# The convolution branch's output projection as four Strassen pairs instead of sixteen plain products

## The chip, the cores and the metric

One Trainium2 chip; the kernel runs on one of its cores. The metric is the device time of one execution in microseconds (us); the time given for a kernel is the median of its runs. One further execution is recorded by the hardware profiler, which logs the instructions of each engine and the transfers. Engines: PE (TensorE, matrix products), PEld (its weight loads), DVE (VectorE), ACT (ScalarE), POOL (GpSimd), SP (SyncE, which issues nearly all transfers here).

## The reference, cut to what matters

One encoder block on 1024 tokens with 1024 channels in fp32: two branches, each gated and projected, then merged.

```python
h = rmsnorm(x, norm_w) * (1 + scale) + shift          # [1024 tokens, 1024]
proj = h @ w_in                                       # all branches at once
ya = a_cg * dwconv_centred(a_bg * a_x, conv_a_w)      # convolution branch, width 3
ya = ya * silu(a_z)
ya = ya @ w_pa                                        # the first output projection, "pa"
...                                                   # yb: gated DeltaNet over q, k, v with z
yb = yb @ w_pb                                        # the second, "pb"
merged = sigmoid(gate_a_raw) * ya + sigmoid(gate_b_raw) * yb
x = x + gate * (merged @ w_o)                         # gate: from c @ w_ada, "output gate"
out = rmsnorm(x, final_norm_w)
```

## The kernel before, in words

Everything is kept transposed: a channel block of 128 channels lies on the 128 partitions, the 1024 tokens along the free axis. A matrix product in fp32 is made of three passes in the format fp32r: each operand t is split into hi = round(t) (a copy on ACT) and lo = t - hi (a subtraction on DVE or POOL), and PE adds whi*rhi + whi*rlo + wlo*rhi in PSUM. One such pass for 128 output channels, 128 contraction channels and 512 tokens is one instruction, "a matmul" below.

**Stages.** Up to about 757 us a planner (`sched.run`) orders the gated DeltaNet heads with the projections that feed them. After that the text below is program order on each engine, for ACT, DVE, POOL and SP, until the context `sctx` closes; PE runs its products in the order written too. In turn come the convolution branch in sixteen pairs, the rest of the gate of the second branch (`gb`: two pairs, then `gate_block` 6 and 7 as plain products), pa as plain products, pb as plain products, and the final projection with `w_o`.

**A plain product** (`product`) is 8 contraction blocks by 3 passes = 24 matmuls for one output block and 512 tokens.

**A pair** (class `Pair`) computes two output blocks j0 and j0+1 for both token halves with seven products in place of eight, by Strassen's scheme in Winograd's form. Its weight operands are four quarters `A11, A12, A21, A22` (output block by half of the contraction; the halves are the even and the odd channel blocks, `KORDER`) and their sums `S1` to `S4` (`ADDS`); its right-hand operands are `B11, B21, B22` of h and the sums `T1` to `T4` of h (`RHS`), which stand ready in `hop`. A product is 4 blocks by 3 passes = 12 matmuls, so a pair is 84 instead of 96. `load` fetches the four raw quarters (names `wr_...`), `operand` forms the sums on DVE, `prep` makes hi on ACT, `rest` makes lo on DVE, `product` issues the matmuls, and `after` issues what follows a product: `u2`, `u3`, `e1` are copies or sums of PSUM banks in SBUF, and `consume` takes a finished quarter of the result. S2, S3 and A22 add up in one PSUM bank (pool `pg`), S1 and S4 in one of `pc`, A11 and A12 each have one of `pp`. S3 may add to the bank only after u2 has been read from it, A22 only after u3 has.

**The order of pairs.** `steps` lists pairs bg, ax, cg, az for j0 = 0, 2, 4, 6 and then gb2, gb4, seven products each. In the ordinary order (S2, A11, S1, S3, A12, A22, S4) a pair begins with S2; the first pair has the order A11, A12, S4, S2, S1, S3, A22, the last one S2, S3, S1, A22, A11, A12, S4. In step i the loop issues the loads of the pair of step i+10, `prep` for step i+5, `rest` for step i+4, then the product of step i, then one operation from the list `late`: the three taps of the width-3 convolution per channel block. The early operands and the first two products of bg0 stand in the planner's part (`ps_first_A11`, `ps_first_A12`).

**The channel blocks of ya.** After az, `a` holds a finished block of the branch (`conv * silu(a_z) * a_cg`); it is stored to `y_d` in DRAM. At four steps before the end of the list all eight blocks are fetched into `ylo` and split into `yhi`, `ylo` around gate blocks 6 and 7.

**pa** runs over j = 0..7: weights by `wtile` (hi on ACT, lo on POOL), two products, a multiplication with the stored gate `sga` on DVE, and a store to `m_d`. The same loop fetches the second branch's `yb_d` into `blo`, splits it into `bhi`, `blo`, and forms the output gate: a `tensor_tensor_reduce` on DVE per j, with a fetch of 512 KB of `wadag`.

**pb** runs over j = 0..7: two products, the gate `sgb`, the addition of `m_d`, the split of the result.

Of the kernel before, what the change touches and what calls it, by code (L numbers as in the profile page):

```python
# [8 lines left out]
F32 = mybir.dt.float32  # L9
# [6 lines left out]
P = 128  # L16
# [311 lines left out]
def block(ctx: ExitStack, tc: tile.TileContext, x, c, wada, wadag, badaT, nwT, win, wab, cva, cvq,  # L328
# [860 lines left out]
    def fill():  # L1189
# [100 lines left out]
    class Pair:  # L1290
# [36 lines left out]
        def rest(self, n):  # L1327
            if len(self.ops[n]) < 3:
                return
            hi, lo, t = self.ops[n]  # L1330
            V.tensor_tensor(lo, t, hi.bitcast(F32), ALU.subtract)

        def product(self, n):
            own = self.place and n in ("A12", "S4")
            pl = po if own else BANK[n]
            first = own or pl not in self.banks
            if first:
                self.banks[pl] = bank(pl, f"ps_{self.name}_{n}")
            ps = self.banks[pl]
            hi, lo = self.ops.pop(n)[:2]  # L1340
            for m in range(4):
                for i, (w, r) in enumerate(terms((hi, lo), RHS[n], m)):
                    PE.matmul(ps, w, r, start=first and m == i == 0, stop=m == 3 and i == 2, skip_group_check=True)  # L1343
            self.after(n, ps)

        def temp(self, k, a, b):
            t = self.u[k] = btile(k, f"{k}_{self.name}", 1)
            if b is None:
                S.activation(t, a, AF.Copy)
            else:  # L1350
                V.tensor_tensor(t, a, b, ALU.add)

        def after(self, n, ps):
# [36 lines left out]
    def mixed(name, j0, place):  # L1390
# [7 lines left out]
        def consume(b, half, ps, add):  # L1398
# [18 lines left out]
            if name == "ax":  # L1417
                V.tensor_tensor(x, t, x, ALU.mult)
                if seen[b] == 2:
                    acc = full("a", b)  # L1420
                    late.extend((acc, b, j0 + b, i) for i in range(3))
                return
# [50 lines left out]
    for n in ("A11", "A12"):  # L1473
        steps.pop(0)
        pairs[0].after(n, early[n])
    steps[AHEAD - 1][0].prep(steps[AHEAD - 1][1])
    for i, (p, n) in enumerate(steps):
        if i + AHEAD + 5 < len(steps) and not steps[i + AHEAD + 5][0].raw:
            steps[i + AHEAD + 5][0].load()
        if i + AHEAD < len(steps):  # L1480
            q, k = steps[i + AHEAD]
            q.prep(k)
        if i + AHEAD <= len(steps):
            q, k = steps[i + AHEAD - 1]
            q.rest(k)
        p.product(n)
        if late:
            conv3(*late.pop(0))
        if i + 4 == len(steps):
            tctx.close()  # L1490
            yp = ctx.enter_context(tc.tile_pool(name="yp", bufs=1, reuse_waits="tile", side="right"))
            yhi = [yp.tile([P, T], F32R, name=f"yhi{k}") for k in range(KT)]
            ylo = [yp.tile([P, T], F32R, name=f"ylo{k}") for k in range(KT)]
            ws = [wtile(win[G_B + j], f"gb{j}") for j in (6, 7)]
            for k in range(KT):
                Q.dma_start(ylo[k].bitcast(F32), y_d[k])

# [15 lines left out]
    bp = bctx.enter_context(tc.tile_pool(name="bp", bufs=1, reuse_waits="tile"))
    bhi = [bp.tile([P, T], F32R, name=f"bhi{k}") for k in range(KT)]
    blo = [bp.tile([P, T], F32R, name=f"blo{k}") for k in range(KT)]
    with tc.tile_pool(name="bs", bufs=2, reuse_waits="tile") as bs, tc.manual_schedule(engines=others):
        sgs, wts = [], []

        def fetch(j):
            sgs.append(bs.tile([P, T], F32, tag="sg", name=f"sga{j}"))  # L1520
            Q.dma_start(sgs[j], sga_d[j])
            wts.append(bs.tile([P, T], F32, tag="wadag", name=f"wadag{j}"))
            Q.dma_start(wts[j], wadag[j])
            Q.dma_start(blo[j].bitcast(F32), yb_d[j])

        sc_t = bs.tile([P, T], F32, tag="sc", name="sc_g", bufs=1)
        Q.dma_start(sc_t, sc_d.to_broadcast([P, T]))
        fetch(0)
        for j in range(8):
            if j < 7:  # L1530
                wpas.append(wtile(wpa[j + 1], f"pa{j + 1}"))
                fetch(j + 1)
            sg, wt = sgs[j], wts[j]
            for half in range(2):
                ps = product(wpas[j], yhi, ylo, half, f"pa{j}")
                V.tensor_tensor(sg[:, ch(half, 512)], ps, sg[:, ch(half, 512)], ALU.mult)
# [28 lines left out]
    pair = []  # L1565
    with tc.tile_pool(name="ms", bufs=2, reuse_waits="tile", side="right") as ms:
        for j in range(8):
# [5 lines left out]
            Q.dma_start(sg, sgb_d[j])  # L1573
            for half in range(2):
# [73 lines left out]
def layout(inputs):  # L1648
# [5 lines left out]
    def cols(w, order=tuple(range(8))):  # L1654
# [46 lines left out]
```

## Time and profile before

| | us |
|---|---|
| median of 3 runs | 1402.04 |
| the runs | 1401.67, 1402.04, 1405.6 |
| profiled execution, its own time | 1405.5 |
| its span in the profile | 1403.8 |
| mean granted TensorE clock | 0.994 of full |
| PE busy | 1366.0 (97%) in 8498 matmuls |
| DVE, ACT, POOL busy | 860.7, 613.9, 480.1 |

How to read it. The span reaches from the first to the last instruction that the profiler logged; the execution's time is 1.7 us longer. "Busy" leaves out waits. A row of a timeline gives the start, the duration, the engine, the line of the kernel, the operation, output <- inputs, their shapes, and in brackets the time for which the engine stood idle before it and what ended that. Rows of the waits give the summed idle time, the number of waits and the longest. In a window's row the columns are the window, its length, the busy time of PE, PEld, DVE, ACT and POOL with the number of instructions, the granted TensorE clock, the busy share of the DMA engines and their GB/s. Gate block 7 ends at 1132.3 us, pa at 1219.4, pb at 1307.3.

### The profile page before, as it was taken

Reading aid. Unit: us, or ns where it says so; the run is one execution under the profiler, and the core shown is the slowest. Engines: PE = TensorE matmul, PEld = TensorE weight load, DVE = VectorE, ACT = ScalarE, POOL = GpSimd, SP = SyncE. Lnnn points to the kernel's source line nnn. Section 1 sums busy time; section 2 is a strip of 40 time slices with the busy share of each in tenths; the row PEclk is TensorE's granted clock in tenths of the full one; section 3 lists DMA queues with packets and bytes.
Section 4 is the critical chain, followed back from the end, with each engine's and each line's share of the span. In section 5 each row is a group of like instructions: output and inputs, shape, how many; then the busy total and the mean of one; then the engine's idle time right before and its main releaser. Section 6 shows DMA issues by size and latency. Waiting matters only on the chain.

```text
span 1403.8 us, 22367 instructions
## 1 busy us (share of the span) xinstructions
PE 1366.0 (97%) x8498; PEld 1142.7 (81%) x8498; DVE 860.7 (61%) x1479; ACT 613.9 (44%) x1496; POOL 480.1 (34%) x718
## 2 busy tenths in 40 slices
PE   5899999999999999999998999999999999999998
PEld 5678888897888888888887888888887788888886
DVE  6868175667758685858585776767686344432335
ACT  5447575564647475654535232232324332222211
POOL 2004837573747565675510000000000123455301
PEclk9999999999999999999999999999999999999999
DMA  9325332515033332414223112121211577655502
GB/s 358 98 61 154 113 89 71 151 35 146 31 87 95 83 99 59 123 43 95 62 103 123 60 47 89 46 90 60 90 46 46 199 272 243 227 190 158 180 15 105
DMA packets 124300, 155.96 MB, mean 111 GB/s; under 512 B 74657, under 2 KB 75041, under 8 KB 124194
## 3 DMA queue, kind: packets, MB, share of 16 engines
q1 hardware_dynamic: 123762, 153.24, 34.0%
q8 instruction: 66, 1.08, 0.3%
q10 hardware_dynamic: 432, 1.31, 0.2%
q14 instruction: 40, 0.33, 0.1%
HBM read 125.02 MB, written 29.50 MB: 110 GB/s over the span
## 4 chain that ended last, share of the span: by engine, by line
PE 92%; DVE 4%; DMA 1%; ACT 1%; issue 1%; SPq 0%; POOL 0%; POOLq 0%; ACTq 0%; DVEq 0%
PE pp_ga L214 6%; PE pp_z L214 6%; PE cb L214 6%; PE pp_q L214 5%; PE pp_v L214 5%; PE pp_k L214 5%; PE ps_ax_S L1343 4%; PE ps_cg_S L1343 4%; PE o L214 4%; PE ps_az_S L1343 4%; PE ps_bg_S L1343 3%; PE pp_pb L1261 2%; PE pp_pb L1263 2%; PE pp_pa L1261 2%; PE pp_pa L1262 2%; PE pp_pa L1263 2%
## 5 line engine op out<-in xcount | busy, mean ns | idle before, releaser
L1253 POOL TENSOR_TENSOR wl_gb<-wr_gb,wh_gb 128x512 fp32r<-128x512 f32 x4 | 5.6, 1416 | 352.2 <-ACT wh_gb L1252 352.2
L322 POOL TENSOR_TENSOR E<-E,et 128x30 f32<-128x30 f32 (+7 forms) x240 | 118.7, 495 | 16.8
L322 POOL TENSOR_TENSOR et<-E 128x30 f32<-128x30 f32 (+7 forms) x240 | 109.9, 458 | 29.0 <-DMA E<-s 12.4
L322 DVE SCALAR_TENSOR_TENSOR S<-S,exps,cb 128x128 f32<-128x128 f32 x96 | 29.6, 344 | 60.3 <-PE cb L214 59.5
L322 ACT ACTIVATE vw<-cb,cols 128x128 f32<-128x128 f32 x112 | 36.2, 364 | 68.0 <-PE cb L214 67.7
L214 PE MATMUL pp_z<-hhi,wh_z 128*128 128x512 f32 x128 | 52.8, 412 | 0.0
L214 PE MATMUL pp_z<-hlo,wh_z 128*128 128x512 f32 x128 | 52.7, 412 | 0.0
L214 PE MATMUL pp_z<-hhi,wl_z 128*128 128x512 f32 x128 | 52.7, 412 | 0.0
L214 PE MATMUL pp_ga<-hhi,wl_ga 128*128 128x512 f32 x128 | 51.8, 404 | 0.0
L214 PE MATMUL pp_ga<-hhi,wh_ga 128*128 128x512 f32 x128 | 51.6, 403 | 0.0
L214 PE MATMUL pp_ga<-hlo,wh_ga 128*128 128x512 f32 x128 | 51.4, 402 | 0.0
L1261 PE MATMUL pp_pb<-bhi,wh_pb 128*128 128x512 f32 x128 | 50.4, 394 | 0.0
L322 DVE SCALAR_TENSOR_TENSOR r<-cb,negeg,vp 128x128 f32<-128x128 f32 x112 | 34.5, 345 | 25.6 <-PE cb L214 25.1
L1263 PE MATMUL pp_pb<-bhi,wl_pb 128*128 128x512 f32 x128 | 50.2, 392 | 0.0
L1261 PE MATMUL pp_pa<-yhi,wh_pa 128*128 128x512 f32 x128 | 49.8, 389 | 0.0
L1263 PE MATMUL pp_pa<-yhi,wl_pa 128*128 128x512 f32 x128 | 49.8, 389 | 0.0
L1262 PE MATMUL pp_pa<-ylo,wh_pa 128*128 128x512 f32 x128 | 49.8, 389 | 0.0
L1253 POOL TENSOR_TENSOR wl_pa<-wr_pa,wh_pa 128x512 fp32r<-128x512 f32 x16 | 27.4, 1726 | 65.4 <-ACT wh_pa L1252 58.4
L1262 PE MATMUL pp_pb<-blo,wh_pb 128*128 128x512 f32 x128 | 49.7, 388 | 0.0
L322 ACT ACT_TABLE_LOAD x38 | 48.8, 1283 | 1.4 <-PEq L1696 0.8
L322 DVE SCALAR_TENSOR_TENSOR vT<-xpad,cvq_t,vT 128x1024 f32<-128x1024 f32 x32 | 48.8, 1525 | 0.3
L214 PE MATMUL pp_q<-hhi,wl_q 128*128 128x512 f32 x112 | 45.0, 401 | 2.5 <-issue 2.5
(887 smaller groups left out, 4377.8 us busy)
## 6 DMA issues: line engine op xcount, KB each, us to landing
wada<-in_wada SPq DMA_DIRECT2D x16, 512.0 KB, 8.2
D<-gr_d SPq DMA_DIRECT2D x16, 512.0 KB, 6.4
wr_bg<-in_win SPq DMA_DIRECT2D x18, 256.0 KB, 2.9
xt<-in_x SPq DMA_DIRECT2D x8, 512.0 KB, 8.9
wr_k<-in_win SPq DMA_DIRECT2D x16, 256.0 KB, 2.7
wr_q<-in_win SPq DMA_DIRECT2D x16, 256.0 KB, 2.6
wr_v<-in_win SPq DMA_DIRECT2D x16, 256.0 KB, 2.9
wr_ga<-in_win SPq DMA_DIRECT2D x16, 256.0 KB, 2.7
```

What stands on the lines that cost most here:

```text
L214: getattr(self.pe, what)(out, *ins, **kw)
L322: self._sched.record(self._name, lambda: real(*args, **kw), outs, ins, cost, extra, table, op == "memset", port)
L1253: G.tensor_tensor(lo[:, ch(q, 512)], raw, hi[:, ch(q, 512)].bitcast(F32), ALU.subtract)
L1261: PE.matmul(ps, wh, mhi[k][:, sl], start=i == 0, stop=False)
L1262: PE.matmul(ps, wh, mlo[k][:, sl], start=False, stop=False)
L1263: PE.matmul(ps, wl, mhi[k][:, sl], start=False, stop=i == KT - 1)
L1343: PE.matmul(ps, w, r, start=first and m == i == 0, stop=m == 3 and i == 2, skip_group_check=True)
```

## The change

pa becomes four pairs over the two weight blocks each, with right-hand operands made of ya instead of h. Six things change in the code:

1. `y_sum`: after each az pair, four subtractions of 128x512 on DVE, one per step by way of `late`, form T1 to T4 for two channel blocks of ya; they are written over the finished `c` tiles and stored to `t_d`.
2. The pa operands: B11, B21, B22 and T2 (16 pieces of 256 KB) are fetched where `ylo` was fetched before, the 12 pieces of T1, T3, T4 after gate block 7, into the tiles of h that gate block 7 has read. Each is split as before.
3. pa's 28 steps run in the manner of `steps`, with the first pair in the order "first", the last in "last", and DVE forming the lo parts that POOL formed. `look_ahead(pa_steps, 7)` is to load the second pair's weights ahead of gate block 7; step 7 after the exchange of neighbours is `A22` of the first pair, whose weights are there already, so the second pair's weights are loaded in the loop's first step.
4. The b operands are fetched as pa's operands come free and split in the last six steps.
5. The output gate's reductions and the fetches of `wadag` move from the pa loop to the pb loop.
6. In all pairs: u2 has two buffers; the first pair's S4 has its PSUM bank in `pc` instead of `po`; the first two steps of the list issue their product ahead of the prep of later steps; `rest` drops its raw operand.

```diff
+    t_d = dr.tile([4, 2, P, T], F32, name="t_d")
...
         def product(self, n):
             own = self.place and n in ("A12", "S4")
-            pl = po if own else BANK[n]
-            first = own or pl not in self.banks
+            key = pl = BANK[n]
+            if own:
+                key, pl = n, pc if self.place == "first" and n == "S4" else po
+            first = key not in self.banks
...
-            t = self.u[k] = btile(k, f"{k}_{self.name}", 1)
+            t = self.u[k] = btile(k, f"{k}_{self.name}", 2 if k == "u2" else 1)
...
-                del outs["c", b], outs["a", b]
+            if sum(seen) == 4:
+                late.extend(partial(y_sum, j0 // 2, i, *[outs.pop((n, b)) for n in ("a", "c") for b in range(2)])
+                            for i in range(1))
...
+    def y_sum(m, i, a0, a1, c0, c1):
+        r11, r12, r21, r22 = (t[:, ch(h, 512)] for t in (a0, a1) for h in range(2))
+        t1, t3, t2, t4 = (t[:, ch(h, 512)] for t in (c0, c1) for h in range(2))
+        V.tensor_tensor(*((t1, r12, r11), (t3, r22, r12), (t2, r22, t1), (t4, r21, t2))[i], ALU.subtract)
+        if i % 2:
+            Q.dma_start(t_d[m, i // 2], (c0, c1)[i // 2])
+        if i < 3:
+            late.insert(0, partial(y_sum, m, i + 1, a0, a1, c0, c1))
...
     for i, (p, n) in enumerate(steps):
-        if i + AHEAD + 5 < len(steps) and not steps[i + AHEAD + 5][0].raw:
...
+        look_ahead(steps, i + AHEAD + 5)
+        if i < 2:
+            p.product(n)
+        for k in (range(AHEAD - 1, AHEAD + 2) if i == 1 else (i + AHEAD,) if i else ()):
+            advance(steps, k)
+        if i > 1:
+            p.product(n)
...
+            look_ahead(pa_steps, 0)
+            for i4, n4 in enumerate(("B11", "B21", "B22", "T2")):
+                for m in range(4):
+                    fetch_operand(n4, m, yp.tile([P, T], F32R, tag=f"y{4 * i4 + m}", ..., bufs=1))
...
     gate_block(6, ws[0])
-    wpas = [wtile(wpa[0], "pa0")]
-    for k in range(3, KT):
-        split(yhi[k], ylo[k])
+    look_ahead(pa_steps, 7)
+    pas[1].extra()
+    for n in ("B22", "T2"):
+        for m in range(4):
+            split(*yop[n][m])
+    for k in range(AHEAD):
+        advance(pa_steps, k)
     gate_block(7, ws[1])
+    for i4, n in enumerate(("T1", "T3", "T4")):
+        for m in range(4):
+            p, k = order[4 * i4 + m]
+            fetch_operand(n, m, hp.tile([P, T], F32R, tag=f"h{p}{k}", ..., bufs=1))
...
+    for i, (p, n) in enumerate(pa_steps):
+        look_ahead(pa_steps, i + AHEAD + 5)
+        advance(pa_steps, i + AHEAD)
+        for _ in range(2):
+            if todo:
+                n4, m = todo.pop(0)
+                split(*yop[n4][m])
+        p.product(n)
...
+        if i >= len(pa_steps) - 6:
+            for k in ((0,), (1,), (2, 3), (4,), (5, 6), (7,))[i - len(pa_steps) + 6]:
+                split(bhi[k], blo[k])
...
-            for half in range(2):
-                ps = product(wpas[j], yhi, ylo, half, f"pa{j}")
-                V.tensor_tensor(sg[:, ch(half, 512)], ps, sg[:, ch(half, 512)], ALU.mult)
...
-                V.tensor_tensor_reduce(wt, wt, sc_t, 1.0, badaT_t[:, 16 + j : 17 + j], ...)
-                split(bhi[j], blo[j])
...
         for j in range(8):                                  # pb
...
+            V.tensor_tensor_reduce(wt, wt, sc_t, 1.0, badaT_t[:, 16 + j : 17 + j], ...)
```

Where instructions stand, place 1: ACT in the first pair, bg0, before. `whS_...` and `whiA_...` are hi parts made for the pair ax0, `e_bg` and `u_bg` copies of PSUM banks of bg0.

```order
L1324 ACTIVATE whS_bg_8170<-S_bg_8168 128x512
L1349 ACTIVATE e_bg_8174<-ps_first_A_8043 128x512
L1324 ACTIVATE whS_ax_8189<-S_ax_8187 128x512
L1324 ACTIVATE whiA_ax_8206<-wr_ax_8181 128x512
L1349 ACTIVATE u_bg_8222<-ps_bg_S_8209 128x512
L1324 ACTIVATE whiA_ax_8206<-S_ax_8185 128x512
```

The same place now:

```order
L1326 ACTIVATE whS_bg_8171<-S_bg_8169 128x512
L1354 ACTIVATE e_bg_8175<-ps_first_A_8044 128x512
L1354 ACTIVATE u_bg_8212<-ps_bg_S_8199 128x512
L1326 ACTIVATE whS_ax_8220<-S_ax_8218 128x512
L1326 ACTIVATE whiA_ax_8224<-wr_ax_8182 128x512
L1326 ACTIVATE whiA_ax_8224<-S_ax_8216 128x512
```

`u_bg` has moved ahead of the two hi parts for ax0.

Place 2: DVE at the end of az0 and the start of bg2, before. `t_az` and `a` end the branch's block, `S_bg`, `wloA_bg` are made for bg2.

```order
L1424 TENSOR_TENSOR t_az_8724<-t_az_8724,c_8538 128x512
L1425 TENSOR_TENSOR a_8431<-t_az_8724,a_8431 128x512
L1331 TENSOR_TENSOR wloA_bg_8709<-wr_bg_8522,whiA_bg_8708 128x512
L1308 TENSOR_TENSOR S_bg_8745<-wr_bg_8522,S_bg_8616 128x512
L1331 TENSOR_TENSOR wloA_bg_8709<-wr_bg_8518,whiA_bg_8708 128x512
L1351 TENSOR_TENSOR u_bg_8766<-ps_bg_S_8732,e_bg_8764 128x512
```

The same place now:

```order
L1429 TENSOR_TENSOR t_az_8725<-t_az_8725,c_8539 128x512
L1430 TENSOR_TENSOR a_8432<-t_az_8725,a_8432 128x512
L1443 TENSOR_TENSOR c_8539<-a_8432 128x512
L1333 TENSOR_TENSOR wloA_bg_8710<-wr_bg_8523,whiA_bg_8709 128x512
L1443 TENSOR_TENSOR c_8539<-a_8411,a_8432 128x512
L1310 TENSOR_TENSOR S_bg_8749<-wr_bg_8523,S_bg_8617 128x512
L1333 TENSOR_TENSOR wloA_bg_8710<-wr_bg_8519,whiA_bg_8709 128x512
L1356 TENSOR_TENSOR u_bg_8770<-ps_bg_S_8734,e_bg_8768 128x512
```

Two of the four subtractions of `y_sum` (L1443) stand ahead of the sum `S_bg` and of `u_bg`.

Place 3: ACT from the sigmoids of gate block 7 (`xpad1`) on, before.

```order
L1467 ACTIVATE xpad1_119<-pp_gb7_0_10845 128x512
L1467 ACTIVATE xpad1_119<-pp_gb7_1_10871 128x512
L1252 ACTIVATE wh_pa1_10940<-wr_pa1_0_10942 128x512
L1252 ACTIVATE wh_pa1_10940<-wr_pa1_1_10946 128x512
L1499 ACTIVATE bhi0_10912<-blo0_10920 128x1024
```

The same place now; `yop_T1_0` to `yop_T1_3` are the four pieces of T1, `whS2_pa2` the first operand of the second pair.

```order
L1484 ACTIVATE xpad1_120<-pp_gb7_0_10923 128x512
L1484 ACTIVATE xpad1_120<-pp_gb7_1_10949 128x512
L1326 ACTIVATE whiS1_pa0_10919<-S3_pa0_11008 128x512
L1546 ACTIVATE yop_T1_0_10976<-yop_T1_0_10976 128x512
L1546 ACTIVATE yop_T1_1_10978<-yop_T1_1_10978 128x512
L1354 ACTIVATE e1_pa0_11029<-ps_pa0_A11_11016 128x512
L1326 ACTIVATE whS2_pa2_11035<-S2_pa2_11033 128x512
L1546 ACTIVATE yop_T1_2_10980<-yop_T1_2_10980 128x512
L1546 ACTIVATE yop_T1_3_10982<-yop_T1_3_10982 128x512
L1326 ACTIVATE whA22_pa0_11059<-wr_pa011_10713 128x512
```

The hi parts of T1's last two pieces stand behind `whS2_pa2`, and that needs the second pair's raw weights. On SP these are the last of what gate block 7 is followed by:

```order
L1543 DMA yop_T4_0_10992<-t_d_86 128x512
L1543 DMA yop_T4_1_10994<-t_d_86 128x512
L1543 DMA yop_T4_2_10996<-t_d_86 128x512
L1543 DMA yop_T4_3_10998<-t_d_86 128x512
L1319 DMA wr_pa210_11000<-in_wpa 128x512
L1319 DMA wr_pa211_11002<-in_wpa 128x512
L1319 DMA wr_pa200_11004<-in_wpa 128x512
L1319 DMA wr_pa201_11006<-in_wpa 128x512
```

Ahead of these rows stand gate block 7's store and the eight pieces of T1 and T3.

More of the change, by code (lines that the diff above doesn't have):

```diff
@@ L1 @@
+from functools import partial
 from contextlib import ExitStack, contextmanager
@@ L1420, in consume @@
                     acc = full("a", b)
-                    late.extend((acc, b, j0 + b, i) for i in range(3))
+                    late.extend(partial(conv3, acc, b, j0 + b, i) for i in range(3))
                 return
@@ L1475, in block @@
         pairs[0].after(n, early[n])
-    steps[AHEAD - 1][0].prep(steps[AHEAD - 1][1])
-    for i, (p, n) in enumerate(steps):
-        if i + AHEAD + 5 < len(steps) and not steps[i + AHEAD + 5][0].raw:
[L1479 to L1496, printed above, removed]
+    yop = {n: [None] * 4 for n in hop}
@@ new lines, in block, with merged_pair, load_gates, consume @@
+    pas = []
+    def merged_pair(j0, place):
+        gates = []
+        def load_gates():
+            for b in range(2):
+                gates.append(btile("out", f"sga{j0 + b}", 4, (P, T)))
+                Q.dma_start(gates[b], sga_d[j0 + b])
+        seen = [0, 0]
+        def consume(b, half, ps, add):
+            g = gates[b][:, ch(half, 512)]
+            if add is not None:
+                t = btile("tmp", f"t_pa{j0}{b}{half}", 2)
+                V.tensor_tensor(t, ps, add, ALU.add)
+                ps = t
+            V.tensor_tensor(g, ps, g, ALU.mult)
+            seen[b] += 1
+            if seen[b] == 2:
+                Q.dma_start(m_d[j0 + b], gates[b])
+        return Pair("pa", j0, consume, place, [wpa[j0], wpa[j0 + 1]], yop, load_gates)
@@ new lines, in block, with look_ahead, advance @@
+    pas = [merged_pair(j, {0: "first", 6: "last"}.get(j)) for j in range(0, 8, 2)]
+    pa_steps = [(p, n) for p in pas for n in p.order]
+    for i in (6, len(pa_steps) - 8):
+        pa_steps[i : i + 2] = pa_steps[i + 1], pa_steps[i]
+    def look_ahead(steps, i):
+        if i < len(steps) and not steps[i][0].raw:
+            steps[i][0].load()
+    def advance(steps, k):
+        if k < len(steps):
+            steps[k][0].prep(steps[k][1])
+        if 0 < k <= len(steps):
+            steps[k - 1][0].rest(steps[k - 1][1])
@@ L1544, in block @@
-    mhi, mlo = yhi, ylo
+    for i, (p, n) in enumerate(steps):
+        look_ahead(steps, i + AHEAD + 5)
[5 more added lines that the diff above has]
+            p.product(n)
+        if late:
+            late.pop(0)()
+        if i + 4 == len(steps):
+            assert not late
+            tctx.close()
+            yp = ctx.enter_context(tc.tile_pool(name="yp", bufs=1, reuse_waits="tile", side="right"))
+            ws = [wtile(win[G_B + j], f"gb{j}") for j in (6, 7)]
+            look_ahead(pa_steps, 0)
+            for i4, n4 in enumerate(("B11", "B21", "B22", "T2")):
+                for m in range(4):
+                    fetch_operand(n4, m, yp.tile([P, T], F32R, tag=f"y{4 * i4 + m}", name=f"yop_{n4}_{m}", bufs=1))
@@ new lines, in block, with fetch_b @@
+    places = order[12:] + order[4:8] + order[0:4] + order[8:12]
+    bhi, blo = [], []
+    def fetch_b(k):
+        for i, l in enumerate((bhi, blo)):
+            p, kk = places[2 * k + i]
+            l.append(hp.tile([P, T], F32R, tag=f"h{p}{kk}", name=f"b{('hi', 'lo')[i]}{k}", bufs=1))
+        Q.dma_start(blo[k].bitcast(F32), yb_d[k])
+    todo = [(n, m) for n in ("T1", "T3", "T4") for m in range(4)]
+    fetched = {"S3": (2, 3), "S1": (4, 5), "A22": (6, 7)}
+    for i, (p, n) in enumerate(pa_steps):
[6 more added lines that the diff above has]
+        p.product(n)
+        if i in (8, 15):
+            pas[i // 7 + 1].extra()
+        if i == len(pa_steps) - 10:
+            for k in range(2):
+                fetch_b(k)
+        if p is pas[-1] and n in fetched:
+            for k in fetched[n]:
+                fetch_b(k)
+        if i >= len(pa_steps) - 6:
+            for k in ((0,), (1,), (2, 3), (4,), (5, 6), (7,))[i - len(pa_steps) + 6]:
+                split(bhi[k], blo[k])
```

80 lines of the change are left out of this document (38 added, 42 removed).

## The prediction

> **What bounds the kernel now.** I read the page's head and the chain of waits first, then windows for the stages that change.
>
> ```profile
> span 1403.8 us, 22367 instructions
> PE 1366.0 (97%) x8498; PEld 1142.7 (81%) x8498; DVE 860.7 (61%) x1479; ACT 613.9 (44%) x1496; POOL 480.1 (34%) x718
> PE 92%; DVE 4%; DMA 1%; ACT 1%; issue 1%; SPq 0%; POOL 0%; POOLq 0%; ACTq 0%; DVEq 0%
> 861.90:939.40 77.50, 77.50 (x338) 63.15 (x337) 55.11 (x82) 22.48 (x39) 0.00 (x0) 1.00 0.20 69
> 1110.30:1132.30 22.00, 22.00 (x98) 18.06 (x97) 9.47 (x12) 11.72 (x17) 5.63 (x4) 1.00 0.94 356
> 1132.30:1219.40 87.10, 87.10 (x385) 72.11 (x385) 44.75 (x43) 21.18 (x31) 28.97 (x17) 1.00 0.70 239
> 1219.40:1307.30 87.90, 87.90 (x386) 72.10 (x386) 24.23 (x31) 23.35 (x39) 48.31 (x38) 1.00 0.55 180
> ```
>
> PE is busy 97% of the span and 92% of the chain. The windows are four pairs in their steady run (28 products of 12 matmuls), gate blocks 6 and 7, pa, and pb: PE has no gap in any of them, at full clock. So fewer matmuls save time one for one, as long as PE doesn't begin to wait; each new wait costs its whole length. What matters is therefore 48 matmuls saved against the places where a 128x512 operand comes late. The sum is made against the profiled execution's 1405.5; the median of the runs is 1402.04, 3.5 lower, and I move the result by that.
>
> **Term F, the matmuls of pa.** 384 become 336 = 28 products. The window of four pairs has 28 in 77.5 us, 2.77 each, against 87.1 for pa now: **-9.6**. At pa's own 87.1/384 = 0.227 per matmul it would be 76.2 and -10.9; I take the pairs' rate, since these are the same 12-matmul products.
>
> **Term A, the first pair (bg0).** This is what stands there before:
>
> ```profile
> PE ps_bg_S L1343 <- ACT u_bg L1349: 3.3, 1, 3.3
> PE ps_bg_S L1343 <- DVE sz L322: 0.9, 1, 0.9
> 767.04 0.58 ACT L1349 ACTIVATE e_bg<-ps_first_A 128x512 f32<-128x512 f32 x1
> 769.09 0.69 DVE L1308 TENSOR_TENSOR S_ax<-S_ax,wr_ax 128x512 f32<-128x512 f32 x1
> 769.82 0.63 ACT L1324 ACTIVATE whS_ax<-S_ax 128x512 fp32r<-128x512 f32 x1 [2.20 <-DVE S_ax L1308]
> 770.87 0.58 ACT L1349 ACTIVATE u_bg<-ps_bg_S 128x512 f32<-128x512 f32 x1
> 771.50 4.57 PE ps_bg_S L1343 x12
> 781.62 2.76 PE ps_ax_A L1343 x12
> 768.00:771.50 3.50, 0.24 (x2) 0.00 (x0) 2.46 (x5) 1.68 (x4) 0.00 (x0) 0.99 0.61 217
> 771.50:775.00 3.50, 3.50 (x9) 2.78 (x10) 3.40 (x6) 0.47 (x1) 0.00 (x0) 0.52 0.01 2
> ```
>
> S4 waits 0.9 for its `po` bank. S3 waits 3.3, to 771.50, for the copy u_bg, which ACT holds behind whS_ax, which waits 2.20 for a DVE sum. And S3 then takes 4.57 instead of 2.76, at a granted clock of 0.52 after 3.3 us of idleness: 1.8 more. Now u_bg stands right behind e_bg: 767.04 + 0.58 and another copy, so S3 starts at about 768.2, and S4's bank is free. But DVE's two adds into u2 (0.6 each) now stand ahead of S_ax, so whS_ax ends about 1.3 later and ax0's first product, which follows S3 at 771.0, waits 0.9 to 1.2; A22 waits about 0.7 for u3. A22 would end at about 778.3 instead of 781.5, where ps_ax_A follows now: **-3.2** (-2 if both small waits grow by half a microsecond, -4 if neither comes).
>
> The Trainium skill ("TensorE: Matmul & The Clock Gate", "What's actually happening") has PE fall to half clock after an idle window of 3.4 us that runs freely and returns after a busy one; the row at 0.52 agrees. By it, whether a wait below that length costs anything beyond itself depends on where it falls in the window: estimated, 0 to 1.7 us more.
>
> **Term D, u2 with two buffers.** In gb4, the "last" pair, u2's copy has to wait for the tile:
>
> ```profile
> PE ps_gb_S L1343 <- ACT u_gb L1349: 1.4, 1, 1.4
> PE ps_gb_S L1343 <- DVE u_gb L1351: 0.4, 1, 0.4
> 1092.80 0.60 ACT L1349 ACTIVATE u_gb<-ps_gb_S 128x512 f32<-128x512 f32 x1 [4.34 <-DVE gb L1447]
> ```
>
> ACT stood 4.34 us until DVE had read the old u2 (L1447 is the gate's consumption). With a second buffer the 1.4 goes: **-1.5**, with a little for the restart. Nothing was late behind it.
>
> **Term B, y_sum's sixteen subtractions.** DVE is busy 55.1 of 77.5 us there, so 16 x 0.6 have room on the average. What counts is where they stand. Two of each four stand ahead of the next pair's S_bg and u_bg, at its start:
>
> ```profile
> 840.67 0.69 DVE L1425 TENSOR_TENSOR a<-t_az,a 128x512 f32<-128x512 f32 x1
> 841.28 0.69 DVE L1331 TENSOR_TENSOR wloA_bg<-wr_bg,whiA_bg 128x512 fp32r<-128x512 f32 x1
> 841.88 0.69 DVE L1308 TENSOR_TENSOR S_bg<-wr_bg,S_bg 128x512 f32<-128x512 f32 x1
> 843.22 0.58 ACT L1349 ACTIVATE e_bg<-ps_bg_A 128x512 f32<-128x512 f32 x1
> 843.83 0.69 DVE L1351 TENSOR_TENSOR u_bg<-ps_bg_S,e_bg 128x512 f32<-128x512 f32 x1 [0.67 <-ACT e_bg L1349]
> 845.04 0.63 PE L1343 MATMUL ps_bg_S<-sums_D,whS_bg 128*128 128x512 f32 x2
> ```
>
> A DVE operation that needs nothing of the one before starts 0.60 later (841.28 to 841.88); I add 0.13 for one that does (t_az to a, elsewhere 0.73). The first subtraction reads `a` just written: 0.73 + 0.60 = 1.33 on the way to u_bg, directly and by way of ACT, which makes whS_bg from S_bg ahead of e_bg. u_bg ends at 844.52 and S3 starts at 845.04: slack 0.5. So each of the three bg starts costs 1.33 - 0.46 = 0.87, and gb2's, which already waits 0.4, the whole 1.33: 3 x 0.87 + 1.33 = **+3.9**. It is 0 if ACT's order leaves e_bg unharmed and DVE's 0.67 idle takes it, +5 if each takes all 1.33. The eight stores and the fetches cost nothing: loads are issued ten steps, 27.7 us, ahead, and the DMA engines are 0.20 busy there.
>
> **Term G, the first pa pair.** Gate block 7 ends at T0 = 1132.3. SP then has its store, which waits for the sigmoid:
>
> ```profile
> 1134.46 1.06 ACT L1467 ACTIVATE xpad<-pp_gb 128x512 f32<-128x512 f32 x2
> 1135.55 0.33 SPq L1468 DMA_DIRECT2D sgb_d<-xpad  x1
> wr_ax<-in_win SPq DMA_DIRECT2D x16, 256.0 KB, 2.7
> 1116.00:1120.00 4.00, 4.00 (x19) 3.27 (x18) 2.35 (x4) 3.88 (x5) 0.00 (x0) 1.00 1.01 385
> 1120.00:1124.00 4.00, 4.00 (x19) 3.30 (x18) 1.83 (x2) 1.28 (x3) 0.00 (x0) 1.00 1.01 401
> ```
>
> In the new order the sigmoid stands first, so I set the store at T0 + 1.9. Behind it come the 12 pieces of T1, T3, T4 and the second pair's raw weights. Its third quarter is the 17th piece of 256 KB, counting the store as two: 4.46 MB, at the 385 to 401 GB/s of the fetches of `ylo` 11.3 us, and some 2.0 fixed (a lone 256 KB lands in 2.7): T0 + 15. (By 358 GB/s, the limit that the Trainium skill gives under "DMA: Bandwidth & Descriptors", Specifications, it would be an estimated 12.5 us and a sum 1.2 higher; the rows show 401, and I keep them.) Then S2_pa2 on DVE and whS2_pa2 on ACT, T0 + 16.4; and only behind that, in ACT's order, the hi parts of T1's last two pieces, which PE needs in the middle of its fifth product, at T0 + 4.5 x 2.77 = 12.5. PE waits to about T0 + 17.1: 4.6. Behind it DVE is late: till u3 of the first pair it has 22 operations of 0.60 and 3 dependent ones, 13.6, from T0 + 17.1 on; u3 ends at T0 + 30.8 and A22, due after seven products at T0 + 19.4, starts at 30.9. That wait contains the first one: 11.5, and 0.8 for one stretch at half clock (half of A's 1.8): **+12.3**. The low end is +4.6, if DVE's backlog doesn't reach u3; the high end +14.5, for two such stretches of 1.8 and little else.
>
> **Term H, from pa to pb.** Each split of b takes DVE one operation of 128x1024:
>
> ```profile
> 1130.79 6.02 DVE L1500 TENSOR_TENSOR ylo<-ylo,yhi 128x1024 fp32r<-128x1024 f32 x5 [8.96 <-ACT yhi L1499]
> 1140.04 2.10 DVE L1500 TENSOR_TENSOR blo<-blo,bhi 128x1024 fp32r<-128x1024 f32 x1
> 1139.13 1.93 POOL L1253 TENSOR_TENSOR wl_pa<-wr_pa,wh_pa 128x512 fp32r<-128x512 f32 x1 [0.31 <-ACT wh_pa L1252]
> ```
>
> 1.2 each (6.02/5), 2.1 when POOL subtracts at the same time. Let E be the end of the last pa product. A11 of the last pair ends at E - 5.5; from it DVE has the copy and seven additions and multiplications, about to E, then blo4, two for the gate, blo5, blo6, two for the gate, blo7: four of 1.2 and four of 0.6 = 7.3. pb0 takes 24 matmuls of 0.227 and wants its last lo part at E + 5.0: **+2.8**, with half a microsecond for blo6 on the way (0 if POOL keeps off and the gates' work comes earlier, +4.5 with 2.1 in place of 1.2 twice).
>
> **At nothing:** the first 16 splits of 128x512 lie beside the gate blocks, where DVE is busy 9.5 and ACT 11.7 of 22 us; pa's later pairs run at 20 DVE operations (12.5 us) per 19.4; the reductions, 8 x 2 us, move into pb, where DVE is busy 24 of 88. If they stood ahead of a gate multiplication, a PSUM bank would come late; each pb product lasts 5.4, so there is room.
>
> **Sum:** -9.6 - 3.2 - 1.5 + 3.9 + 12.3 + 2.8 = +4.7. 1405.5 becomes 1410.2; on the medians 1402.04 becomes **1406.7**, 0.34% slower. About 0.3%, 4.2 us, is what a measurement of this kernel can tell from no change: 1397.8 to 1406.2.
>
> **The rivals.**
> 1. *The second pair's weights come in time* (faster). If the third quarter landed by T0 + 10, whS2_pa2 would be done before T1's last pieces are due, and no backlog would build; G falls away: 1406.7 - 12.3 = 1394.4. For it: fetches may overlap the store more than I reckon. Against: 4.46 MB by T0 + 10 asks for 4.46/6.1 = 730 GB/s, and no row has more than 401. 0.15, mainly because ACT may not run as late as its place in the order says.
> 2. *The small delays are absorbed* (no change). Term B at 0, by DVE's idle 0.67, and H at 0: 1406.7 - 6.7 = 1400.0. For it: both rest on half-microseconds of slack. 0.20.
> 3. *The half clock spreads* (slower). Each of the three waits of the first pa pair and of pb0 is followed by a slow product, 1.8 each as at 771.5, of which G has 0.8: 3 x 1.8 + 1.8 - 0.8 = +6.4: 1413. It decides where a wait is longer than about 3.3 us. 0.13.
>
> **How the numbers follow.** The forecast has 0.52. It lies half a microsecond beyond the bound of no change, so of its 0.52 some 0.33 are slower and 0.19 the same; its own range is 1401 to 1411. With rival 1 faster (0.14, a hundredth of it the same), rival 2 the same and rival 3 slower: faster 0.14, same 0.40, slower 0.46. The range reaches from 1396, where rival 1 begins, to rival 3's 1413.
>
> **What the changed profile would show.** F: 336 matmuls of pa, about 2.77 a product from the second pair on. A: S3 of bg0 at about 768, no row with clock 0.52 there. G: a wait of PE's at S1 of pa0 for ACT's hi part of T1, and a longer one at its A22 for DVE's u3; raw weights of pa2 landing 15 us after gate block 7. B: three short waits of S3 in bg2, bg4, bg6, and one in gb2. H: a wait of pb0's first product for blo6 or blo7. I would be wrong most of all if u3 of pa0 came at its time although whS2_pa2 didn't.

## The result

| | median us | runs | ratio to the kernel before, 95% interval |
|---|---|---|---|
| before | 1403.28 | 1401.67 to 1405.6, 4 runs | |
| changed | 1417.05 | 1416.29 to 1419.85, 4 runs | 1.0093 [1.0077, 1.0109] |
| forecast | 1406.7 | stated range 1396 to 1413 | |

The change makes the kernel slower by 0.9%, and not by the 0.3% forecast: the direction was right, the size was not, and the time lies outside the range. The page of the changed kernel, its first lines and its chain:

```profile
span 1418.1 us, 22459 instructions
...
PE 1362.4 (96%) x8450; PEld 1135.1 (80%) x8450; DVE 919.1 (65%) x1583; ACT 632.4 (45%) x1535; POOL 462.8 (33%) x702
...
PE 85%; DVE 8%; DMA 3%; ACT 2%; issue 2%; POOL 0%; SPq 0%; POOLq 0%; ACTq 0%; DVEq 0%
```

PE has 48 matmuls less, but only 3.6 us less of busy time, and the chain now runs through DVE, DMA and ACT for 13% of a longer span. PE's waits from the convolution branch on, as total, number and longest:

```profile
PE ps_pa_S L1348 <- ACT yop_T L1546: 8.3, 1, 8.3
PE ps_pa_S L1348 <- DVE u_pa L1356: 4.7, 1, 4.7
PE pp_pb L1264 <- DVE blo L1547: 4.2, 3, 3.6
PE ps_bg_S L1348 <- DVE u_bg L1356: 2.5, 4, 0.7
PE ps_gb_S L1348 <- DVE u_gb L1356: 1.4, 1, 1.4
PE ps_bg_S L1348 <- ACT u_bg L1354: 1.0, 1, 1.0
PE ps_pa_S L1348 <- ACT u_pa L1354: 0.9, 1, 0.9
PE ps_ax_S L1348 <- ACT whS_ax L1326: 0.7, 1, 0.7
```

The long ones stand where the forecast put them; the 0.9 for `u_pa` it did not have. Windows of the changed kernel show what it cost beyond the waits: pa, its last three pairs, pb, and the three stretches behind the long waits.

```profile
1130.85:1227.07 96.22, 82.33 (x337) 65.52 (x336) 62.46 (x93) 35.75 (x57) 4.58 (x2) 0.93 0.53 189
1172.00:1227.00 55.00, 55.00 (x240) 44.91 (x240) 39.54 (x56) 21.23 (x30) 4.58 (x2) 1.00 0.54 193
1227.07:1321.80 94.73, 90.50 (x387) 73.26 (x386) 47.52 (x55) 23.91 (x40) 56.54 (x39) 0.98 0.64 216
1151.70:1155.00 3.30, 3.23 (x6) 1.77 (x6) 3.25 (x6) 3.30 (x7) 0.00 (x0) 0.50 0.00 1
1166.40:1172.00 5.60, 5.58 (x13) 4.43 (x14) 2.58 (x5) 0.00 (x0) 0.00 (x0) 0.50 0.00 0
1237.00:1240.60 3.60, 3.51 (x8) 2.82 (x9) 0.03 (x1) 0.63 (x1) 1.28 (x1) 0.53 0.79 258
```

Behind each of the waits of 8.3, 4.7 and 3.6 us TensorE ran at half clock, for some 3.4 to 5.9 us.

To compare kernels I take three lengths of each profiled execution, between the starts of first matmuls: the convolution branch with the gate blocks (from bg0's first to pa's first), pa (to pb's first), pb (to the final projection's first). The part ahead of bg0 varies by 6 us between executions, 748.0 to 754.3, with the same code in it, so single spans are not compared. Each length comes from one profiled execution. In the changed kernel, e3 and e6, which have the same instructions in pa but for its last three steps, pa took 96.2, 95.5 and 94.7; so a difference of 1.5 us in pa can be chance.

| kernel | branch and gates | pa | pb | ratio to before, 95% interval |
|---|---|---|---|---|
| before | 380.1 | 87.1 | 89.6 | |
| changed | 379.4 | 96.2 | 96.3 | 1.0093 [1.0077, 1.0109] |
| e1 weights first | 379.4 | 88.9 | 96.2 | 1.0043 [1.0026, 1.0060] |
| e2 splits first | 379.4 | 90.8 | 96.8 | 1.0054 [1.0034, 1.0074] |
| e3 sums later | 375.1 | 95.5 | 96.7 | 1.0056 [1.0038, 1.0075] |
| e4 mends only | 375.1 | 87.2 | 89.7 | 0.9963 [0.9948, 0.9978] |
| e5 T first | 379.4 | 84.8 | 96.2 | 1.0022 [1.0011, 1.0033] |
| e6 b first | 379.4 | 94.7 | 96.0 | 1.0095 [1.0080, 1.0111] |
| e7 all four | 375.1 | 83.6 | 95.2 | 0.9993 [0.9984, 1.0003] |
| e8 both holds | 375.1 | 79.5 | 95.0 | 0.9959 [0.9944, 0.9974] |
| e9 hold last | 375.1 | 84.5 | 94.0 | 0.9987 [0.9972, 1.0003] |
| e10 hold first | 375.1 | 79.5 | 95.3 | 0.9956 [0.9942, 0.9971] |
| e11 gate later | 375.1 | 79.5 | 91.5 | 0.9922 [0.9906, 0.9937] |

The changed kernel's 14.3 us in the profiled executions are -0.7 in the branch, +9.1 in pa, +6.7 in pb and -0.8 in the rest (0.6 of it ahead of bg0).

### The profile page after: what moved, and what is told of

Its sections match the earlier page's. It is cut to its first block, busy times and chain, and to the rows that moved or that the text cites. A ratio compares the mean times of both kernels' runs of the same rounds, so it can differ in the third digit from the quotient of the medians.

```text
span 1418.1 us, 22459 instructions
## 1 busy us (share of the span) xinstructions
PE 1362.4 (96%) x8450; PEld 1135.1 (80%) x8450; DVE 919.1 (65%) x1583; ACT 632.4 (45%) x1535; POOL 462.8 (33%) x702
## 4 chain that ended last, share of the span: by engine, by line
PE 85%; DVE 8%; DMA 3%; ACT 2%; issue 2%; POOL 0%; SPq 0%; POOLq 0%; ACTq 0%; DVEq 0%
PE pp_ga L215 6%; PE pp_z L215 6%; PE pp_q L215 6%; PE cb L215 6%; PE pp_v L215 6%; PE pp_k L215 5%; PE ps_cg_S L1348 4%; PE o L215 4%; PE ps_ax_S L1348 4%; PE ps_pa_S L1348 3%; PE ps_az_S L1348 2%; PE pp_pb L1264 2%; PE ps_bg_S L1348 2%; PE fo L1688 2%; PE fo L1687 2%; PE fo L1689 2%
## 5 line engine op out<-in xcount | busy, mean ns | idle before, releaser
L323 POOL TENSOR_TENSOR E<-E,et 128x30 f32<-128x30 f32 (+7 forms) x240 | 122.5, 510 | 16.8
L1255 POOL TENSOR_TENSOR wl_pb<-wr_pb,wh_pb 128x512 fp32r<-128x512 f32 x16 | 25.1, 1577 | 128.1 <-DMA blo<-yb_d 104.7
L323 ACT ACTIVATE vn<-cb,cols 128x128 f32<-128x128 f32 x128 | 41.4, 372 | 10.4 <-PE cb L215 10.4
L215 PE MATMUL pp_q<-hhi,wh_q 128*128 128x512 f32 x112 | 45.6, 407 | 0.0
L215 PE MATMUL pp_v<-hhi,wl_v 128*128 128x512 f32 x112 | 45.4, 406 | 0.0
```

Of the source, the lines that this page charges most:

```text
L215: getattr(self.pe, what)(out, *ins, **kw)
L323: self._sched.record(self._name, lambda: real(*args, **kw), outs, ins, cost, extra, table, op == "memset", port)
L1255: G.tensor_tensor(lo[:, ch(q, 512)], raw, hi[:, ch(q, 512)].bitcast(F32), ALU.subtract)
```

## The experiments

Each kernel was timed in turn with the kernel before on the same chip.

**e1, the second pair's weights ahead of gate block 7's store.**

```diff
-    look_ahead(pa_steps, 7)
+    look_ahead(pa_steps, 6)
```

> Edit: the second pair's weights are loaded ahead of gate block 7's store (step index 6 instead of 7), so the 12 T fetches no longer stand before them. Theory L (the late raw weights of pa2 start the stall): the wait of 8.3 us in S1 of pa0 goes or shrinks below 1; T1 lands at about T0+8.5, DVE then has some 22 operations up to u3, 13.6 us, so A22 still waits about 4 us; of the 18.7 us that pa took beyond 28 x 2.77, 11 to 13 go: 1404 to 1406. Rival O (the stall is DVE's amount of work, the weights only the name of the last one to come): the wait moves to T1's own landing and to u3, at most 5 us are gained: 1412 or more.

Between the two: pa lost 7.3 us, not 11 to 13 and not under 5. The wait in S1 falls from 8.3 to 0.9; the one for u3 stays. Waits of PE in this kernel's pa, and the DVE row at T1's arrival:

```profile
PE ps_pa_S L1348 <- DVE u_pa L1356: 4.7, 1, 4.7
...
PE ps_pa_S L1348 <- ACT u_pa L1354: 2.0, 1, 2.0
...
PE ps_pa_S L1348 <- ACT yop_T L1546: 0.9, 1, 0.9
```

```profile
1141.87 1.37 DVE L1547 TENSOR_TENSOR yop_T<-yop_T 128x512 fp32r<-128x512 f32 x2 [6.45 <-ACT yop_T L1546]
```

So the late weights caused the first wait, and not the second. DVE stands idle 6.45 us for T1, and then its queue runs without a stop until u3.

**e2, the T splits ahead of prep, the weights left late.**

```diff
-        advance(pa_steps, i + AHEAD)
         for _ in range(2):
             if todo:
                 n4, m = todo.pop(0)
                 split(*yop[n4][m])
+        advance(pa_steps, i + AHEAD)
```

> Edit: in pa's loop the two splits of T pieces are issued ahead of prep and rest; the weights stay late. Theory L: T1's last pieces are split at about 1142 and S1 of pa0 no longer waits, but T3's first piece now stands behind whS2_pa2, which comes at 1150.5, so S3 waits to about 1151.5, 7 us instead of 8.3 + 0.9, and A22 for u3 little earlier; gain 2 to 4 us: 1413 to 1415. Rival A (ACT's and DVE's order is the cause, any order with T first mends it): both waits go, gain 9 or more: 1408 or less.

pa is 5.4 shorter, the ratio 0.4% lower: near theory L. The wait went to S3, as foretold, but was 10.0 and not 7: S3 may add to its bank only after the copy `u2`, and in ACT's order this copy stands behind `whS2_pa2` and six more operations:

```profile
PE ps_pa_S L1348 <- ACT u_pa L1354: 10.0, 1, 10.0
```

It is one wait of 10.0 instead of 8.3 + 0.9 + 4.7, and followed by one slow stretch instead of two. Order alone doesn't remove the stall.

**e3, y_sum two steps later.**

```diff
+                late.extend([lambda: None] * 2)
                 late.extend(partial(y_sum, ...))
```

> Edit: y_sum's four subtractions begin two steps later than in the change, behind the u2 of the next pair. The changed profile has three waits of 0.7 for u_bg and one of 1.4 for u_gb. Theory B (these are the two subtractions that stand ahead of S_bg and u_bg): the waits go but gb2's last 0.4: gain 3.1, 1413.5 to 1414.5. Rival: they come from elsewhere (loads, the mends) or move to the next products: no gain, 1417.

The branch is 4.3 shorter, 379.4 to 375.1, and so is every kernel with this edit. Of those four waits none is left, gb2's 0.4 of before included; only the first pair still has its small ones. Term B is shown: 16 subtractions of 0.6 us cost 4.3 us by their place alone, and nothing at another, for the branch is as long in e4, which has no such subtraction.

**e4, the mends of the pairs alone,** put into the kernel before (the edits are those of the diff in `product`, `temp` and the first two steps).

> Edit: the kernel before with the mends of the pairs alone (two buffers of u2, S4's bank in pc, the first two products ahead of the prep, raw dropped). From the changed profile the first pair ended 3.6 us earlier and gb4's wait of 1.4 is gone: theory: 5.0 faster than before, 1397 to 1399 where before is 1402 to 1403. Rival: given back by later waits in the convolution branch: no change.

As expected: 0.9963, 5.2 us. The branch is 5.0 shorter. What PE still waits for, in the whole kernel from bg0 on:

```profile
PE ps_bg_S L1346 <- ACT u_bg L1352: 1.0, 1, 1.0
PE ps_ax_S L1346 <- ACT whS_ax L1324: 0.7, 1, 0.7
PE ps_bg_S L1346 <- DVE u_bg L1354: 0.4, 1, 0.4
```

**e5, T ahead of gate block 7's store and of two gates,** with the weights first.

```diff
-    pas[1].extra()
...
     gate_block(7, ws[1])                # its store moved
...                                      # fetch_operand of T1, T3, T4
+    store()
+    pas[1].extra()
```

> Edit: as with the weights first, and the 12 T fetches also ahead of gate block 7's store and of the gates sga2, sga3 on SP, so that they no longer wait for the sigmoid and 1 MB of gates. With the weights first A22 of pa0 still waits 4.7 for u3, because DVE stood idle 6.5 us until T1 had landed (10 us after gate block 7) and then works through its queue without a gap. Theory D (DVE's queue starts too late, by T's landing): T1 lands some 5 us earlier, the queue ends in time, pa shrinks from 88.9 to 78 to 80: 9 us faster than with the weights first, 1402 where before is 1404.6. Rival: DVE has too much to do in that stretch however early T comes, or the DMA engines are full: A22 still waits over 3, gain below 4.

4.1 us in pa and 0.2% in the ratio: near the rival, whose bound was 4. T1 comes earlier, and A22 waits exactly as long, now as the only wait of pa:

```profile
PE ps_pa_S L1348 <- DVE u_pa L1356: 4.7, 1, 4.7
```

**e6, the last b splits ahead of the last products' gate work,** in the changed kernel.

```diff
+        if i >= len(pa_steps) - 3:
+            split_b()
         p.product(n)
```

> Edit to the changed kernel alone: in pa's last three steps the b splits are issued ahead of the product's consumption, so that blo4 to blo7 no longer stand behind the last pair's six gate operations. Theory H (pb0 waits because DVE's order has the gates ahead of blo5 to blo7): the 4.2 us of waits in pb0 fall below 1 and the half clock after them goes: pb from 94.7 to 88 to 89, 6 us gained: 1411. Rival: the b pieces land late or POOL at the same time slows DVE: the wait stays above 3, gain below 2.

The theory failed: nothing was gained (1.0095). The wait for blo fell to 2.6, but A11's seven operations still stood ahead of them, and 2.3 us of new waits for pb's weights, on ACT and POOL, took the place.

**e7, all four edits together.**

> The changed kernel with all four edits: weights first, T first, sums two steps later, b splits first. If the terms add, 16 + 3.5 + 6 below the changed kernel: 1391 to 1393 where before is 1404.6, and 7 below the mends alone: then 336 matmuls in place of 384 are worth their 9.6 us less small waits. If a common limit (DVE or the fetches) stood behind all of them, the sum stays 1398 or more, no better than the mends alone.

Same as before, 0.9993, and not 1391: pa still has the wait of 4.7, and pb is hardly shorter. The DVE queue in this kernel, from T1's arrival to u3, the first and the last of 27 operations, and the matmul that waits:

```profile
1131.40 1.36 DVE L1547 TENSOR_TENSOR yop_T<-yop_T 128x512 fp32r<-128x512 f32 x2 [2.66 <-ACT yop_T L1546]
...
1149.24 0.68 DVE L1356 TENSOR_TENSOR u_pa<-ps_pa_S,e_pa 128x512 f32<-128x512 f32 x1
```

```profile
1150.07 1.19 PE L1348 MATMUL ps_pa_S<-yop_T,whA_pa 128*128 128x512 f32 x2 [4.67 <-DVE u_pa L1356]
```

DVE starts on T 5.6 us after gate block 7 (1125.8) and then has no gap over 0.7 us in 17.8 us. What holds A22 is the DVE work that stands ahead of u3 in that stretch.

**e8, e9, e10: work held back on DVE.** In e10 the gate multiplications of A12 and S1 in pa0 wait until u3 is out, and the second pair's first two sums go ahead of T's splits. In e9 all gate work of the last pair waits until the last b split is out. e8 has both. The core of each:

```diff
+            elif n == "A12" and first and self.rhs is not hop:
+                self.held.append((0, 0, ps, u["e1"]))      # consumed behind u3 (e10)
...
+    pas[1].operand("S2")                                   # ahead of the T splits (e10)
...
+    for finish in pas[-1].held:                            # behind blo7 (e9)
+        finish()
```

> All four edits, and two more: on DVE the first pa pair's gate work for A12 and S1 (4 operations) is issued behind u3 and the second pair's first sums (2) ahead of T's splits; and in the last pa pair all gate work is issued behind the last b split. Theory: what is left of pa's stall is DVE's queue up to u3 (26 operations without a gap) and of pb0's the seven operations of A11 in front of blo5 to blo7. Then A22's wait goes from 4.7 to about 0.7 with no half clock after it (7 us), and pb0's from 3 to below 1 (3 us with the clock): 10 us below the four edits, 1393 to 1395 where before is 1405. Rival: both waits only pass to the next operand, as with b first: gain below 4.

> Of the two holds only the one in the last pa pair. Theory: 3 us below the four edits, pb's stretch from 92.8 to 89 to 90. Rival (POOL's wl of pb slows the b splits from 1.2 to 2.3 each, and blo7 is late in any order): no gain.

> Of the two holds only the one in the first pa pair. Theory: A22's wait falls from 4.7 to about 0.7 and the half clock after it goes: pa's stretch from 83.6 to 78 to 79, 5 to 7 us below the four edits. Rival: u3 is held by something else than the number of operations ahead of it: the wait stays above 3.

e10 did what was expected: pa from 83.6 to 79.5, A22's wait to 1.2, no half clock, 5 us. e9 gained nothing that can be told (0.9987 against 0.9993, pb 94.0): the wait for blo is gone altogether, but three for pb's weights stand in its place, 3.2 together, 37 to 62 us into pb. e8 is e10 and no more. Its wait in pb and two windows of pb, which runs from 1208.7 on:

```profile
PE pp_pb L1265 <- POOL wl_pb L1255: 2.4, 2, 2.1
```

```profile
1222.00:1232.00 10.00, 10.00 (x45) 8.24 (x44) 3.60 (x5) 1.57 (x3) 5.63 (x4) 1.00 0.98 358
1232.00:1242.00 10.00, 10.00 (x45) 8.19 (x45) 9.72 (x11) 3.58 (x6) 6.99 (x5) 1.00 0.92 348
```

The DMA engines are nearly full from 1222 to 1242: the fetches of wadag, which the change moved here, run beside m_d, sgb and the weights. The wait of 2.1 comes later, at 1253.81. On ACT and POOL stand ahead of it:

```profile
1250.51 0.62 ACT L1254 ACTIVATE wh_pb<-wr_pb 128x512 fp32r<-128x512 f32 x1
...
1252.48 2.19 POOL L1682 TENSOR_TENSOR mr<-mr,sgb 128x512 f32<-128x512 f32 x1 [1.29 <-issue]
...
1254.63 1.27 POOL L1255 TENSOR_TENSOR wl_pb<-wr_pb,wh_pb 128x512 fp32r<-128x512 f32 x1
```

The weights had landed, since ACT had their hi part ready at 1251.13. On POOL the lo part stands behind the addition `mr`, which took 2.19 here and 1.29 at 1242.69. Ahead of it the lo part could have started at 1251.2, when POOL's operation before ended, and by an estimate from these rows it would have been ready before 1253.81.

**e11, the output gate's fetches two turns later,** on top of e8. The reductions on DVE and the fetch of `sc_t`, which they read, move with them.

```diff
-            wt = ms.tile([P, T], F32, tag="wadag", name=f"wadag{j}")
-            Q.dma_start(wt, wadag[j])
...
+            for g in {2: (0,), 3: (1,), 4: (2, 3), 5: (4, 5), 6: (6, 7)}.get(j, ()):
+                wt = ms.tile([P, T], F32, tag="wadag", name=f"wadag{g}")
+                Q.dma_start(wt, wadag[g])
+                V.tensor_tensor_reduce(wt, wt, sc_t, ...)
```

> The kernel with both holds, and in the pb loop the eight fetches of wadag (512 KB each) with their reductions begin two turns later. With both holds no wait for blo is left, but pb still takes 93.1 instead of 87.9: PE waits 2.1 and 0.3 for POOL's lo of pb's weights about 45 us into pb, and runs at half clock after it, while the DMA engines were 0.92 to 0.98 busy 15 to 35 us into pb. Theory: the reductions' fetches, moved here by the change, crowd out m_d, sgb and the weights at pb's start, POOL's in-order queue then runs late: pb goes to 88 to 89, 4 to 5 us gained, 1393 to 1394 where before is 1404.8. Rival: pb starts late anyway because m_d of the last pair is stored only at its end: gain below 2.

1393.60 where before is 1405.34: 0.9922, faster than both kernels and than the mends alone. pb is 3.5 shorter, and what is left of waits in pb is small:

```profile
PE pp_pb L1265 <- POOL wl_pb L1255: 0.6, 1, 0.6
PE pp_pb L1263 <- ACT wh_pb L1254: 0.6, 1, 0.6
```

The time is the one expected, but the cause is not shown. The DMA engines are still 0.96 busy between 1220 and 1242, so their load as such was not what held POOL. And the edit changed a second thing, the order on POOL, where the same lo part now stands ahead of the addition:

```profile
1247.70 2.28 POOL L1255 TENSOR_TENSOR wl_pb<-wr_pb,wh_pb 128x512 fp32r<-128x512 f32 x1
1249.94 1.29 POOL L1678 TENSOR_TENSOR mr<-mr,sgb 128x512 f32<-128x512 f32 x1
```

e7 and e10 have POOL's order of e11 with the fetches where e8 has them, and wait at most 0.5 for this lo part; but there PE comes to it later, by the wait for blo. By e8's rows the order is the nearer cause. What the fetches cost by themselves was not tried.

## Why the prediction was right and wrong

**Terms A, D, B** came out to half a microsecond. The branch was to change by -3.2 - 1.5 + 3.9 = -0.8 and changed by -0.7; taken apart by e4 and e3, the mends are -5.0 (forecast -4.7) and y_sum +4.3 (forecast +3.9), so that the two errors cancel in the sum.

**Term F** was right: in 55.0 us of the last three pairs stand 240 matmuls, which is 2.75 a product, with no gap.

**Term G** was forecast as 12.3 and measured 96.2 - 77.5 = 18.7. The mechanism was the one foretold, seen here row by row in the changed kernel:

```profile
1149.02 0.69 DVE L1310 TENSOR_TENSOR S_pa<-wr_pa,wr_pa 128x512 f32<-128x512 f32 x1 [7.67 <-DMA wr_pa<-in_wpa]
...
1150.54 0.63 ACT L1326 ACTIVATE whS_pa<-S_pa 128x512 fp32r<-128x512 f32 x1 [9.42 <-DVE S_pa L1310]
...
1151.74 1.52 PE L1348 MATMUL ps_pa_S<-yop_T,whiS_pa 128*128 128x512 f32 x2 [8.26 <-ACT yop_T L1546]
...
1165.59 0.68 DVE L1356 TENSOR_TENSOR u_pa<-ps_pa_S,e_pa 128x512 f32<-128x512 f32 x1
...
1166.42 1.19 PE L1348 MATMUL ps_pa_S<-yop_T,whA_pa 128*128 128x512 f32 x2 [4.73 <-DVE u_pa L1356]
```

Two steps of it failed. The landing of the weights: T0 + 18.2 (T0 is now 1130.85, the start of pa) instead of T0 + 15. The step "4.46 MB behind the store, at 385 to 401 GB/s" left out what was already in the queue. SP and the DMA engines then:

```profile
1127.81 1.57 SPq L1502 DMA_DIRECT2D sga<-sga_d  x2
...
1133.65 0.32 SPq L1485 DMA_DIRECT2D sgb_d<-xpad  x1
```

```profile
1130.85:1133.60 2.75, 2.75 (x13) 2.25 (x12) 2.59 (x6) 2.62 (x6) 0.00 (x0) 1.00 0.98 399
1133.60:1149.00 15.40, 9.88 (x43) 7.69 (x42) 1.91 (x3) 2.36 (x5) 0.00 (x0) 0.98 0.97 330
```

Two gates of 512 KB were issued at 1127.8, the engines were full when the store came at T0 + 2.8 (not 1.9), and from there they moved 330 GB/s, 5.1 MB up to 1149.0 where 4.46 had been counted. (The Trainium skill's "DMA: Bandwidth & Descriptors", Specifications, gives 358 GB/s per core; the trace passed it before the store, 399, and stayed below it after, so the page's figure would have been the better one for this stretch.) The waits became 8.3 + 0.9 + 4.7 = 13.9 instead of 11.5.

The larger step was the clock: "0.8 for one stretch at half clock". Beyond its waits pa lost 18.7 - 13.9 = 4.8, in two stretches at 0.50: 3.5 us from 1151.74 on and 5.9 us from 1166.42 on cost half their length, 4.7. My own forecast had a first wait of 4.6 and then more, both longer than the 3.3 whose 1.8 I had quoted, so this price could have been had from the row; rival 3 had it.

**Term H** was forecast as 2.8 and measured 6.6: waits of 4.2 and 2.4 beyond them, 1.7 of it for 3.4 us at half clock. That no clock was charged is the same step. The waits are longer because DVE's operations take longer where POOL is at work. DVE's and POOL's rows of the changed kernel at the start of pb:

```profile
1227.22 1.22 DVE L1547 TENSOR_TENSOR blo<-blo,bhi 128x1024 fp32r<-128x1024 f32 x1
...
1233.05 1.78 DVE L1512 TENSOR_TENSOR sga<-t_pa,sga 128x512 f32<-128x512 f32 x1
1234.75 2.28 DVE L1547 TENSOR_TENSOR blo<-blo,bhi 128x1024 fp32r<-128x1024 f32 x1
```

```profile
1233.01 1.27 POOL L1255 TENSOR_TENSOR wl_pb<-wr_pb,wh_pb 128x512 fp32r<-128x512 f32 x1 [3.41 <-DVE t_pa L1510]
1234.24 1.71 POOL L1638 TENSOR_TENSOR wol<-wor,woh 128x512 fp32r<-128x512 f32 x1
```

The same split takes 1.22 where it began before POOL's subtraction (the next one on POOL starts at 1227.80) and 2.28 where POOL had begun before it; I had 1.2 in the sum and 2.1 only in the range.

**At nothing: the reductions in pb.** In the changed kernel no wait is put down to them, but blo's wait comes first there. With that gone (e8, e9) PE waits 2.1 for POOL, and moving the reductions and their fetches (e11) took 3.5 us off pb. How much of this is theirs is open, because e11 changed the order on POOL as well.

**The rivals.** Rival 1 had priced the whole of G on the second pair's weights. e1 shows that they are worth 7.3, and e5 and e10 that T's late landing (4.1) and then the DVE work ahead of u3 (4.1) are two more causes, each hidden behind the one before. Rival 2 didn't come. Rival 3, which had 0.13, is what came on top of the forecast: it priced the clock at 6.4 more, and 4.0 in pa and 2.4 in pb were measured. That these totals agree is luck: it counted four stretches of 1.8, and there were three, one of them over half as long again. With 2.4 and 1.4 of longer waits pa and pb are 10.2 above their terms. The profiled executions differ by 14.3 where 4.7 was forecast, 9.6 too much, since the stages outside took 0.8 less.

## What to carry to other kernels

When a forecast contains a wait, price what follows the wait too: here the three long waits cost another 1.7, 2.9 and 1.7 us of slow matmuls, more than half of the error. Behind a stalled engine look for the next cause before calling the first one the price: the stall of pa had three in a row, and each edit gave a part. A saving of 12% of a stage's matmuls paid (mends alone 0.9963, with the four pairs mended 0.9922) only after DVE's order and the order of the fetches around it were set anew.

## What the runs showed of the hardware that was not expected

A wait of little over 2 us is followed by half clock in some executions and not in others; all waits of 3.3 us and more were. e8 and e9 wait equally long for the same operand in pb, 2.14 and 2.13 us, and only e8's matmuls are slow behind it.

The clock records of the kept traces show why. In each execution the stretches at half clock begin and end on a grid of 3.41 us (the changed kernel's in pa and pb at 1148.39, 1155.22, 1165.46, 1172.29, 1237.14 and 1240.55). What counts is how long PE was idle within one window of this grid, which is the window's length less PE's busy time. e8's wait, the window that holds it and the next:

```profile
1255.95 0.50 PE L1265 MATMUL pp_pb<-bhi,wl_pb 128*128 128x512 f32 x1 [2.14 <-POOL wl_pb L1255]
```

```profile
1253.36:1256.78 3.42, 1.28 (x6) 0.71 (x6) 1.27 (x3) 1.26 (x2) 3.19 (x3) 1.00 0.82 289
1256.78:1260.19 3.41, 3.41 (x10) 2.64 (x9) 1.90 (x3) 0.00 (x0) 1.38 (x2) 0.50 0.89 345
```

e9's two windows around its wait, which ran from 1259.15 to 1261.28 and so reached over a window's end:

```profile
1257.60:1261.02 3.42, 1.55 (x7) 0.94 (x5) 1.60 (x4) 0.63 (x1) 3.20 (x2) 1.00 0.80 261
1261.02:1264.43 3.41, 3.15 (x13) 2.40 (x14) 1.54 (x2) 0.63 (x1) 1.49 (x2) 1.00 0.94 359
```

In e8 all 2.14 us of idleness fall into one window, and the next one runs at 0.50. In e9 1.86 fall into one and 0.26 into the next, and the clock stays at 1.00. So it is in all thirteen profiled executions from 740 to 1385 us: each of the 20 windows at full clock with 2.13 us or more of idleness is followed by one at half clock, and none with 1.86 or less is. A window at half clock is followed by another one if it has 0.82 us or more of idleness itself, and by full clock if it has 0.39 or less. This is why the wait of 4.7 us in pa was dearer than the one of 8.3: it ended 0.96 us into a window at half clock, and a second such window followed.

A window that runs freely is what the Trainium skill has in "TensorE: Matmul & The Clock Gate" ("What's actually happening"). By the page's words a whole window of 3.4 us has to be idle; in these rows 2.13 of 3.41 us were enough. That the price of a wait depends on its place, from nothing to 1.7 us, as the prediction estimated, is what e9 and e8 show. Where between 1.86 and 2.13 the limit lies stays open.
